# Keeping the split output- and query-projection panels in DRAM, and a gate matmul that writes with stride 4

## The chip, the cores and the metric

The kernel runs on one core of a Trainium2 chip. The metric is device microseconds (us) of one execution, as the median of several runs. The core's engines run at the same time, each through its own list of instructions in order: TensorE (PE, with its weight loads PEld), VectorE (DVE), ScalarE (ACT), GpSimd (POOL) and SyncE (SP), which issues most transfers. Transfers of SP and of POOL run on the same 16 DMA engines.

## The reference, cut to what matters

One layer, 1024 tokens of width 1024, float32. Attention in two head groups, then the output projection, then PEER: each token picks 16 of 16384 experts in each of 8 heads by product keys, and sums their one-neuron outputs.

```python
x = x + gt1 * (mixed @ w_out[l])
h2 = rms_norm(x, g_norm_ffn[l]) * (1.0 + sc2) + sh2
query = (ht @ w_query).reshape(t, PEER_HEADS, 2, PEER_HALF)
sub_scores = einsum('thpd,hpkd->thpk', query, sub_keys)
...                      # top 16 of each half, top 16 of their sums
experts = i1 * PEER_N_KEYS + i2
gates = softmax(top_vals)
act = gelu(einsum('td,thkd->thk', xb, expert_down[eb])) * gb
x = x + gt2 * einsum('thk,thkd->td', act, expert_up[eb])
```

## The kernel before, in words

Tokens are cut into block A (five tiles of 128) and block B (three tiles). The block-A tokens go through all 128x128 experts densely ("dense stage"); the block-B tokens gather their own experts' rows (`ring` tiles) beside it.

**Panels.** Products with large weights are made in two float32r halves: `wh` is the rounded weight panel (ACT, `split`), `wl` the rest (DVE, a subtraction in `low`), and `mm3` issues three matmuls for each piece. `Panels` loads a raw panel `wf` (128x1024, 512 KB), splits it one panel ahead of its use, and loads the next when `wf` is free. Two buffers hold `wh` and two `wl`. `w_out` has 8 panels, `w_q` 16; block A and block B each load and split all 24.

**Dense gates.** The dense stage needs, for each expert, the gates of all block-A tokens. Two ways build them:
- Tiles 0 and 1 (`scatter`): POOL adds each gate into the DRAM arrays `gds` by an indirect DMA of 128 single elements, 256 of them. They are issued in order, and each waits for the one issued eight before it. The first needs the first finished group of candidates of block A.
- Tiles 2 to 4 (`gbuild`): one-hot rows `ob` are compared on DVE, copied to `o2` (ACT) or scaled by the gate to `o1` (DVE), multiplied on PE (four matmuls of 128x128 into one PSUM bank), copied to `gt` (ACT), and after every 32 tokens `gt` (2 MB, one buffer) is stored to `gd`. There are 12 such stores.

**Order of the work.** The streams are merged by weights (`mrg`), and a scheduler then orders each engine's list. The stages that matter here: post A and route A (output projection and top-k of block A, beside the projections of block B), attention B, then the last merge, which runs post B, `post_b`, route B and `gbuild` together, then the dense stage, whose PE, DVE and ACT order is the code's own. A group of four experts loads its gates with `loadg`: `gg` from `gds` and `g4` from `gd`. The loads of the first group are issued on POOL, those of the second group on SP.

Of the kernel before, what the change touches and what calls it, by code (L numbers as in the profile page):

```python
# [11 lines left out]
F32 = mybir.dt.float32  # L12
F32R = mybir.dt.float32r
# [3 lines left out]
AF = mybir.ActivationFunctionType  # L17
# [3 lines left out]
P = 128  # L21
T = 1024
D = 1024
# [82 lines left out]
def tile_kernel(ctx: ExitStack, tc: tile.TileContext, x, ccol, w_ada, badac, bgt2, gcols, w_in, w_f, bf_, gout,  # L106
                w_out, w_q, keysT, edown, eup, wdense, gfin, out, dbg=None, stop=None):
    nc = tc.nc
    V, S, G, PE = nc.vector, nc.scalar, nc.gpsimd, nc.tensor
    dma = nc.sync.dma_start  # L110
# [3 lines left out]
    dram = ctx.enter_context(tc.tile_pool(name="dram", bufs=1, space=bass.MemoryType.DRAM))  # L114
# [38 lines left out]
    qsp = dram.tile([8, 3, P, T], F32R, name="qsp")  # L153
    ksp = dram.tile([8, 2, P, T], F32R, name="ksp")
    vsp = dram.tile([8, P, T], F32, name="vsp")
    gd = dram.tile([NPT * P // SB, P, NE * SB], F32, name="gd")
    gds = [dram.tile([NE * P * P, 1], F32, name="gds%d" % i) for i in range(NSC)]
    pidx = cst.tile([P, 1], F32, name="pidx")
# [2 lines left out]
    class Block:  # L161
        def __init__(self, t0, parts):
            self.t0, self.parts = t0, []
            i0 = 0
            for n in parts:
                self.parts.append((i0, n))
                i0 += n
            self.nt = i0
            self.ht = i0 * P
            self.nk = (t0 + i0) * P  # L170
            self.nq = 2 if t0 else 1
# [67 lines left out]
    def defer(fn, n=1):  # L239
        t_ = [n, fn]  # L240
        late.append(t_)
        return t_

    def force(t_):
        if t_ in late:
            late.remove(t_)
            t_[1]()
# [27 lines left out]
    def mrg(*streams, bg=()):  # L275
        live = [[q[0], float(q[1]), 0.0, q[2] if len(q) > 2 else 0] for q in streams + tuple(bg)]
        side = [q[0] for q in bg]
        need = len(streams)
        while need:
            for q in sorted(live, key=lambda q: q[2] / q[1]):  # L280
                c = adv(q)
                if c is None or c >= 0:
                    break
            assert c is None or c >= 0
            if c is None:
                live.remove(q)
                need -= not any(q[0] is g for g in side)
                continue
            q[2] += c
            tick(c)  # L290
            step()
        while late:
            late.pop(0)[1]()
        lead.clear()
# [17 lines left out]
    def split(dst_h, dst_l, src):  # L312
        S.activation(dst_h, src, AF.Copy)
        V.tensor_sub(dst_l, src, dst_h.bitcast(F32))

    class Panels:
        def __init__(self, pool, srcs, bufs=3, eng=V):
            self.eng = eng
            self.pool, self.src, self.bufs = pool, list(srcs), bufs
            self.ld, self.sp = [], []  # L320
            for _ in range(bufs - 1):
                self.load()
            self.split()

        def load(self):
            if self.src:
                w = self.pool.tile([P, D], F32, name="wf", tag="wf", bufs=self.bufs)
                dma(w, self.src.pop(0))
                self.ld.append(w)

        def split(self):
            if self.ld:
                w = self.ld.pop(0)
                wh = self.pool.tile([P, D], F32R, name="wh", tag="wh", bufs=2)
                wl = self.pool.tile([P, D], F32R, name="wl", tag="wl", bufs=2)
                S.activation(wh, w, AF.Copy)

                def low():
                    if self.eng is G:
                        G.tensor_sub(wl, w, wh.bitcast(F32))  # L340
                    else:
                        V.tensor_sub(wl, w, wh.bitcast(F32))

                self.sp.append((wh, wl, defer(low, LW)))
                self.load()

        def get(self):
            wh, wl, t_ = self.sp.pop(0)
            force(t_)
            self.split()  # L350
            return wh, wl

    def mm3(pt, wh, wl, hh, hl, cs, m=P, k0=0, k1=KD):
        for kd in range(k0, k1):
            c = slice(kd * m, (kd + 1) * m)
            PE.matmul(pt, wl[:, c], hh[:, kd, cs], start=kd == 0, stop=False)  # L356
            PE.matmul(pt, wh[:, c], hl[:, kd, cs], start=False, stop=False)  # L357
            PE.matmul(pt, wh[:, c], hh[:, kd, cs], start=False, stop=kd == KD - 1)  # L358
# [656 lines left out]
    def gbuild(ti, gp, alloc):  # L1015
        tp = alloc()
        for n, s_ in enumerate(cols3[ti]):
            PE.transpose(tp[:, n * P:(n + 1) * P], s_, identf)
        ib = gp.tile([P, 2, P], BF, name="ib", tag="ib", bufs=2)
        S.activation(ib, tp[:, :2 * P].rearrange("p (n t) -> p n t", n=2), AF.Copy)  # L1020
        gT = gp.tile([P, P], F32, name="gT", bufs=2)
        S.activation(gT, tp[:, 2 * P:3 * P], AF.Copy)
        io4 = gp.tile([P, P, 4], BF, name="io4", bufs=1)
        if ti == NSC:
            V.tensor_copy(io4, iof[:, :, None].to_broadcast([P, P, 4]))
            gio.append(io4)
        iob = gio[0][:, None].to_broadcast([P, 2, P, 4])

        def onehot(n, t):
            o = gp.tile([P, 2, P, 4], BF, name="ob%d" % n, tag="ob", bufs=3)  # L1030
            ids = ib[:, n, t:t + 8].rearrange("p (q t) -> p q t", t=4)[:, :, None, :]
            V.tensor_tensor(o, iob, ids.to_broadcast([P, 2, P, 4]), OP.is_equal)
            return o.rearrange("p q i t -> p q t i")

        for sb in range(P // SB):
            gt = gp.tile([P, NE, SB], F32, name="gt", tag="gt", bufs=GTB)
            for q in range(SB // 8):
                t = sb * SB + q * 8
                e2 = onehot(1, t)
                o2 = gp.tile([P, 2, 4, P], F32, name="o2", tag="o2", bufs=O2B)  # L1040
                S.activation(o2, e2, AF.Copy)
                e1 = onehot(0, t)
                o1 = gp.tile([P, 2, 4, P], F32, name="o1", tag="o1", bufs=O1B)
                gs = gT[:, t:t + 8].rearrange("p (q t) -> p q t", t=4)[:, :, :, None]
                V.tensor_tensor(o1, e1, gs.to_broadcast([P, 2, 4, P]), OP.mult)
                for q2 in range(2):
                    pg = alloc()
                    for r in range(4):
                        PE.matmul(pg[:, r * P:(r + 1) * P], o2[:, q2, r], o1[:, q2, r], start=True, stop=True)  # L1049
                    c_ = q * 8 + q2 * 4  # L1050
                    S.activation(gt[:, :, c_:c_ + 4].rearrange("p i t -> p t i"), pg.rearrange("p (t i) -> p t i", i=P),  # L1051
                                 AF.Copy)
                    yield GBC
            dma(gd[(ti - NSC) * (P // SB) + sb], gt.rearrange("p i t -> p (i t)"))

# [2 lines left out]
    st_hpa, st_pw, st_hpb, st_xp, st_ad, st_at, st_s3, st_gp = [ExitStack() for _ in range(8)]  # L1058

    def pool(stack, name, bufs=1, **kw):  # L1060
        return stack.enter_context(tc.tile_pool(name=name, bufs=bufs, reuse_waits="tile", **kw))
# [8 lines left out]
    def xtile(p_, b, name):  # L1070
        return p_.tile([P, b.nt, D], F32, name=name, tag="xr")
# [35 lines left out]
    am[0], ax[0] = ALS[0]()  # L1107
    s3p = pool(st_s3, "s3p", side="right")
    wop = [w_out[j] for j in range(KD)] + [w_q[j] for j in range(16)]
    opan = Panels(s3p, wop, bufs=2)  # L1110
    mrg((post(bA, mixA, lambda: xtile(xp, bA, "x1A"), opan), 60, HPB), (ad3, AD3), bg=((pp, PP3), (zr, ZR3)))
    rA = chain(post_b(bA), route(bA, opan))
    mrg((pp, PP4), (ad5, 10), bg=((rA, TOT_RA, HPC), (zr, 20)))
    for st_ in (st_ad, st_hpb, st_pw, st_xp):
# [8 lines left out]
    am[0], ax[0] = ALS[2]()  # L1123
    soft_rs[0] = RS2
    mb = pool(st_at, "mb")
    opan = Panels(s3p, wop, bufs=2)
    hp_[0] = pool(st_hpa, "hpc", 2)
    gp = pool(st_gp, "gp")
    mrg((chain(post(bB, mixB, lambda: xtile(mb, bB, "x1B"), opan), post_b(bB), route(bB, opan)), 150),
        (chain(*[gbuild(ti, gp, ptp) for ti in range(NSC, ND)]), TOT_G))  # L1130
    for st_ in (st_gp, st_hpa, st_at, st_xp, st_s3):
        st_.close()
# [310 lines left out]
```

## Time and profile before

| | |
|---|---|
| three runs | 3127.29, 3130.71 (median), 3133.5 us |
| the profiled execution | 3109.18 us, span 3107.4 us |
| mean granted clock of PE | 0.962 |
| busy: PE, DVE, ACT, POOL | 2864.6, 2561.8, 1213.5, 1587.9 us |

The span is the profiled stretch inside the execution's own time; 1.8 us lie around it. The profiled execution was 21.5 us (0.7%) shorter than the median of the three runs, so a difference read in the trace is added to that median. Busy shares are means over stages with different limits; which engine sets the pace is read stage by stage.

### The profile page before, as it was taken

Reading aid. Unit: us, or ns where it says so; the run is one execution under the profiler, and the core shown is the slowest. Engines: PE = TensorE matmul, PEld = TensorE weight load, DVE = VectorE, ACT = ScalarE, POOL = GpSimd, SP = SyncE. Lnnn points to the kernel's source line nnn. Section 1 sums busy time; section 2 is a strip of 40 time slices with the busy share of each in tenths; the row PEclk is TensorE's granted clock in tenths of the full one; section 3 lists DMA queues with packets and bytes.
Section 4 is the critical chain, followed back from the end, with each engine's and each line's share of the span. In section 5 each row is a group of like instructions: output and inputs, shape, how many; then the busy total and the mean of one; then the engine's idle time right before and its main releaser. Section 6 shows DMA issues by size and latency. Waiting matters only on the chain.

```text
span 3107.4 us, 47293 instructions
## 1 busy us (share of the span) xinstructions
PE 2864.6 (92%) x17213; PEld 2649.5 (85%) x17213; DVE 2561.8 (82%) x5226; ACT 1213.5 (39%) x2098; POOL 1587.9 (51%) x1089
## 2 busy tenths in 40 slices
PE   6999998989988891679999999999999999999997
PEld 4899998988888791679989989899898988999986
DVE  7677645999977693689889899898898988989996
ACT  5566745436767872332312213222122231222312
POOL 0000000077777677026566676665677656657771
PEclk9999999989979996889999999999999999999998
DMA  7998333465435553549999999999999999999995
GB/s 264 298 350 269 124 124 129 138 153 121 105 54 142 157 156 48 166 161 340 349 348 339 339 335 341 351 342 355 328 351 343 335 343 347 346 336 331 348 331 193
DMA packets 385593, 802.43 MB, mean 258 GB/s; under 512 B 66168, under 2 KB 208016, under 8 KB 383824
## 3 DMA queue, kind: packets, MB, share of 16 engines
q0 software_dynamic: 149984, 412.03, 39.4%
q1 hardware_dynamic: 235376, 387.39, 37.0%
q8 instruction: 135, 2.21, 0.3%
q14 instruction: 98, 0.80, 0.1%
HBM read 721.52 MB, written 77.76 MB: 257 GB/s over the span
## 4 chain that ended last, share of the span: by engine, by line
PE 36%; issue 18%; DVE 16%; POOL 14%; DMA 13%; ACT 4%; SPq 0%; POOLq 0%; DVEq 0%; ACTq 0%
DMA ring<-in_eup,e 7%; POOL ring L1193 7%; POOL ring L1206 6%; PE sp L356 3%; PE sp L358 3%; PE sp L357 3%; PE av L683 2%; PE proj L356 2%; PE proj L357 2%; PE proj L358 2%; POOL gds L1011 1%; PE po L1302 1%; PE po L1304 1%; PE po L1303 1%; DMA ring<-in_edown,e 1%
## 5 line engine op out<-in xcount | busy, mean ns | idle before, releaser
L1193 POOL DMA_INDIRECT ring<-in_edown,e x384 | 509.9, 1328 | 391.5 <-DVE ring L1195 223.4
L1206 POOL DMA_INDIRECT ring<-in_eup,e x384 | 573.0, 1492 | 263.6 <-DVE sacc L1211 173.9
L356 PE MATMUL sp<-hT,dl 128*128 128x320 f32 x2048 | 635.2, 310 | 18.0 <-ACT ge L1279 9.7
L357 PE MATMUL sp<-hT,dh 128*128 128x320 f32 x2048 | 634.4, 310 | 0.0
L358 PE MATMUL sp<-hT,dh 128*128 128x320 f32 x2048 | 634.4, 310 | 0.0
L1011 POOL DMA_INDIRECT gds<-g,e x256 | 457.4, 1787 | 312.3 <-DVE i L867 136.6
L1211 DVE SCALAR_TENSOR_TENSOR sacc<-ring,sdot,sacc 128x1024 f32<-128x1024 f32 x381 | 488.7, 1283 | 60.9 <-DMA ring<-in_eup,e 55.6
L1195 DVE SCALAR_TENSOR_TENSOR ring<-ring,sx 128x1024 f32<-128x1024 f32 x384 | 461.3, 1220 | 70.0 <-DMA ring<-in_edown,e 68.9
L356 PEld LDWEIGHTS sp<-hT,dl 128*128 128x128 f32 x2048 | 386.0, 188 | 20.6 <-ACT ge L1279 11.8
L1268 ACT ACTIVATE uh<-wfu 128x1024 fp32r<-128x1024 f32 x128 | 134.8, 1053 | 675.3 <-PE po L1304 675.3
L357 PEld LDWEIGHTS sp<-hT,dh 128*128 128x128 f32 x2048 | 386.1, 189 | 1.2
L358 PEld LDWEIGHTS sp<-hT,dh 128*128 128x128 f32 x2048 | 385.9, 188 | 0.0
L1302 PE MATMUL po<-ul,ch 128*128 128x512 f32 x768 | 303.7, 395 | 18.1 <-DVE accB L1311 10.3
L1279 ACT ACTIVATE ge<-sp 128x320 f32<-128x320 f32 x256 | 110.7, 433 | 498.7 <-PE sp L358 477.9
L1303 PE MATMUL po<-uh,ch 128*128 128x512 f32 x768 | 300.8, 392 | 0.0
L1304 PE MATMUL po<-uh,cl 128*128 128x512 f32 x768 | 300.6, 391 | 0.0
L1303 PE MATMUL pers<-uh,ch 128*128 128x512 f32 x512 | 199.6, 390 | 0.0
L1302 PE MATMUL pers<-ul,ch 128*128 128x512 f32 x512 | 199.5, 390 | 0.0
L1304 PE MATMUL pers<-uh,cl 128*128 128x512 f32 x512 | 199.2, 389 | 0.0
L1302 PEld LDWEIGHTS po<-ul,ch 128*128 128x128 f32 x768 | 145.3, 189 | 56.3 <-DVE accB L1311 18.7
L1049 PE MATMUL tp<-o,o 128*128 128x128 f32 x768 | 102.7, 289 | 93.2 <-ACT gt L1051 89.2
L302 POOL TENSOR_TENSOR i<-ms,mhalf 128x4 f32<-128x4 f32 (+1 forms) x16 | 22.4, 1399 | 324.1 <-DVE ms L300 324.1
(305 smaller groups left out, 6518.4 us busy)
## 6 DMA issues: line engine op xcount, KB each, us to landing
wfd<-in_wdense SPq DMA_DIRECT2D x128, 512.0 KB
wfu<-in_wdense SPq DMA_DIRECT2D x128, 512.0 KB
wa<-in_w_ada SPq DMA_DIRECT2D x96, 256.0 KB
wf<-in_w_in SPq DMA_DIRECT2D x48, 512.0 KB
gd<-gt SPq DMA_DIRECT2D x12, 2048.0 KB
g<-gd SPq DMA_DIRECT2D x31, 768.0 KB
gds<-zt SPq DMA_DIRECT2D x32, 512.0 KB
wf<-in_w_q SPq DMA_DIRECT2D x32, 512.0 KB
```

The source lines that it names most:

```text
L356: PE.matmul(pt, wl[:, c], hh[:, kd, cs], start=kd == 0, stop=False)
L357: PE.matmul(pt, wh[:, c], hl[:, kd, cs], start=False, stop=False)
L358: PE.matmul(pt, wh[:, c], hh[:, kd, cs], start=False, stop=kd == KD - 1)
L1011: G.indirect_dma_start(out=gds[i], out_offset=off, in_=b.g[:, c_:c_ + 1], in_offset=None, compute_op=OP.add)
L1193: G.indirect_dma_start(out=r, out_offset=None, in_=edown, in_offset=bass.IndirectOffsetOnAxis(ap=bs.e[:, c_:c_ + 1], axis=0))
L1195: (V.scalar_tensor_tensor(r, r, 1.0, sx, op0=OP.mult, op1=OP.mult, accum_out=s_[:, j:j + 1]))
L1206: G.indirect_dma_start(out=r, out_offset=None, in_=eup, in_offset=bass.IndirectOffsetOnAxis(ap=bs.e[:, c_:c_ + 1], axis=0))
L1211: (V.scalar_tensor_tensor(acc, r, s_[:, j:j + 1], acc, op0=OP.mult, op1=OP.add))
L1268: S.activation(k.uh, k.wfu, AF.Copy)
L1302: PE.matmul(po, k.ch[:, tcs], k.ul[:, ds_], start=c == 0 and (gi == 0 or not per), stop=False)
L1303: PE.matmul(po, k.ch[:, tcs], k.uh[:, ds_], start=False, stop=False)
L1304: PE.matmul(po, k.cl[:, tcs], k.uh[:, ds_], start=False, stop=c == CG - 1 and (gi == NG - 1 or not per))
```

## The change

A DRAM array `wsp` holds 24 pairs of split panels. Block A's `Panels` stores each `wh` and `wl` there after the split; block B's panels come from a new class, `Kept`, which loads the two halves (512 KB each, three buffers of each) and splits nothing. Apart from that, a gate matmul writes its 128 columns with a step of four elements into the PSUM bank, so that the copy to `gt` reads the bank in order and writes runs of four elements.

```diff
+    wsp = dram.tile([24, 2, P, D], F32R, name="wsp")
...
                 S.activation(wh, w, AF.Copy)
+                kp = self.keep.pop(0) if self.keep else None
 
                 def low():
...
+                    if kp is not None:
+                        for n_, t_ in enumerate((wh, wl)):
+                            dma(kp[n_].bitcast(F32), t_.bitcast(F32))
...
+    class Kept:
+        def __init__(self, pool, srcs, bufs=3):
+            self.pool, self.src, self.bufs, self.ld = pool, list(srcs), bufs, []
+            for _ in range(bufs - 1):
+                self.load()
+
+        def load(self):
+            if self.src:
+                src = self.src.pop(0)
+                t = [self.pool.tile([P, D], F32R, name=n_, tag=n_, bufs=self.bufs) for n_ in ("wh", "wl")]
+                for n_, t_ in enumerate(t):
+                    dma(t_.bitcast(F32), src[n_].bitcast(F32))
+                self.ld.append(t)
+
+        def get(self):
+            self.load()
+            return self.ld.pop(0)
...
-                        PE.matmul(pg[:, r * P:(r + 1) * P], o2[:, q2, r], o1[:, q2, r], start=True, stop=True)
+                        PE.matmul(pg.rearrange("p (i t) -> p i t", t=4)[:, :, r], o2[:, q2, r], o1[:, q2, r],
+                                  start=True, stop=True)
                     c_ = q * 8 + q2 * 4
-                    S.activation(gt[:, :, c_:c_ + 4].rearrange("p i t -> p t i"), pg.rearrange("p (t i) -> p t i", i=P),
-                                 AF.Copy)
+                    S.activation(gt[:, :, c_:c_ + 4], pg.rearrange("p (i t) -> p i t", t=4), AF.Copy)
...
-    opan = Panels(s3p, wop, bufs=2)
+    opan = Panels(s3p, wop, bufs=2, keep=[wsp[j] for j in range(24)])
...
-    opan = Panels(s3p, wop, bufs=2)
+    st_s3.close()
+    opan = Kept(pool(st_s3, "s3k", side="right"), [wsp[j] for j in range(24)], 3)
```

The order of POOL's list is the same in both kernels, and so is the order on PE, DVE and ACT up to post A and through the dense stage. In between, DVE has 24 subtractions fewer and ACT 24 copies fewer, and the scheduler places some rows of the last merge otherwise. On SP, in route A, before (a `w_q` panel among the stores of projection B; `kt` are the keys):

```order
L328 DMA wf<-in_w_q 128x1024
L532 DMA qsp<-pqa 128x384
L532 DMA qsp<-pqb 128x384
L835 DMA kt<-in_keysT 128x128
L532 DMA qsp<-pql 128x384
L504 DMA vsp<-vv 128x384
L328 DMA wf<-in_w_in 128x1024
L545 DMA ksp<-pka 128x384
L545 DMA ksp<-pkb 128x384
```

and at the same place of the change:

```order
L347 DMA wsp<-wh 128x1024
L347 DMA wsp<-wl 128x1024
L329 DMA wf<-in_w_q 128x1024
L555 DMA qsp<-pqa 128x384
L555 DMA qsp<-pqb 128x384
L858 DMA kt<-in_keysT 128x128
L555 DMA qsp<-pql 128x384
L527 DMA vsp<-vv 128x384
L329 DMA wf<-in_w_in 128x1024
L568 DMA ksp<-pka 128x384
L568 DMA ksp<-pkb 128x384
```

Two stores stand directly ahead of each load; the rest is in the same order. On SP at the start of the last merge (post B), before:

```order
L419 DMA x1B<-in_x 128x1024 x3
L1054 DMA gd<-gt 128x4096
L328 DMA wf<-in_w_out 128x1024 x4
L1054 DMA gd<-gt 128x4096
L328 DMA wf<-in_w_q 128x1024 x3
L1054 DMA gd<-gt 128x4096
L328 DMA wf<-in_w_q 128x1024
```

and of the change:

```order
L442 DMA x1B<-in_x 128x1024 x3
L1077 DMA gd<-gt 128x4096
L369 DMA wl<-wsp 128x1024 x2
L369 DMA wh<-wsp 128x1024 x3
L369 DMA wl<-wsp 128x1024 x2
L369 DMA wh<-wsp 128x1024
L1077 DMA gd<-gt 128x4096
L369 DMA wl<-wsp 128x1024
L369 DMA wh<-wsp 128x1024
```

Two loads of 512 KB take the place of one. On SP at the seam from the last merge to the dense stage, before (`gg` waits for the scatters; the two `gd` stores are the 11th and 12th; `wfd` and `wfu` are the dense stage's weights):

```order
L1244 DMA wfu<-in_wdense 128x1024
L1252 DMA gg<-gds_107 128x4x128
L1252 DMA gg<-gds_108 128x4x128
L1054 DMA gd<-gt 128x4096 x2
L1242 DMA wfd<-in_wdense 128x1024
L1254 DMA g_13860<-gd 128x12x128
L1242 DMA wfd<-in_wdense 128x1024
```

and of the change:

```order
L1268 DMA wfu<-in_wdense 128x1024
L1276 DMA gg<-gds_108 128x4x128
L1276 DMA gg<-gds_109 128x4x128
L1077 DMA gd<-gt 128x4096
L1266 DMA wfd<-in_wdense 128x1024 x2
L1077 DMA gd<-gt 128x4096
L1278 DMA g_13865<-gd 128x12x128
```

The two `gg` loads stand ahead of the last two `gd` stores in both; in the change two weight loads come between those stores. On DVE at that seam the subtractions `dl` of the first two experts stand 42 rows behind the last gate product `o` (L1045) before, and directly behind it (L1068) in the change:

```order
L889 MAX v_12810<-sr 128x8
L890 MAX_INDEX i_12811<-v_12810,sr 128x8
L1068 TENSOR_TENSOR o_12688<-ob_12686,gT 128x1024
L978 SCALAR_TENSOR_TENSOR bq<-pos,bq 128x128
L1287 TENSOR_TENSOR dl<-wfd,dh 128x1024 x2
```

## Rows read from the trace of the kernel before

**Rows 1.** Page: the span in 40 equal slices, busy tenths.

```profile
PE   6999998989988891679999999999999999999997
...
POOL 0000000077777677026566676665677656657771
```

**Rows 2.** Busy time by stretch: window, length, PE, PEld, DVE, ACT, POOL, PEclk, DMA share, GB/s.

```profile
930.00:1187.00 257.00, 225.00 (x1493) 213.23 (x1492) 208.35 (x576) 197.46 (x269) 176.85 (x93) 0.95 0.55 152
1187.00:1259.00 72.00, 0.00 (x0) 0.00 (x0) 7.08 (x51) 0.64 (x2) 52.30 (x35) 0.50 0.32 44
```

**Rows 3.** Chain that ended last, around the seam: start, us, what.

```profile
1244.02 5.45 DMA gds<-g,e x2
...
1249.96 8.81 DMA gd<-gt
...
1269.96 7.39 DMA gd<-gt
...
1277.97 10.95 DMA g<-gd
```

**Rows 4.** Timeline of SP's queue at the seam.

```profile
1167.21 0.56 SPq L1244 DMA_DIRECT2D wfu<-in_wdense  x1
1247.08 2.79 SPq L1252 DMA_DIRECT2D gg<-gds  x2
```

**Rows 5.** The scatters (line L1011): times ns min/median/max, first and last start.

```profile
L1011 POOL DMA_INDIRECT gds<-g,e x256: 1539/1552/5116, 614.3 to 1245.9; - x128
```

**Rows 6.** Scatters by stretch: POOL busy (count), PEclk, DMA share, GB/s.

```profile
614.00:690.00 76.00, 56.50 (x33) 0.95 0.55 128
690.00:940.00 250.00, 182.15 (x103) 0.87 0.47 100
940.00:1187.00 247.00, 168.07 (x89) 0.97 0.57 158
1187.00:1246.00 59.00, 49.23 (x33) 0.50 0.22 0
```

**Rows 7.** POOL's waits in those four stretches: total us, times, longest.

```profile
POOL gds L1011 <- DMA gds<-g,e: 11.5, 11, 2.5
...
POOL gds L1011 <- DMA gds<-g,e: 48.2, 34, 3.3
...
POOL gds L1011 <- DMA gds<-g,e: 57.9, 23, 5.8
...
POOL gds L1011 <- issue: 9.8, 32, 0.3
```

**Rows 8.** Timeline of POOL: first and last of eight long waits.

```profile
1010.79 1.63 POOL L1011 DMA_INDIRECT gds<-g,e  x1 [5.51 <-DMA gds<-g,e]
...
1172.17 1.55 POOL L1011 DMA_INDIRECT gds<-g,e  x1 [5.83 <-DMA gds<-g,e]
```

**Rows 9.** Page: DMA issues, KB each.

```profile
gd<-gt SPq DMA_DIRECT2D x12, 2048.0 KB
...
wf<-in_w_q SPq DMA_DIRECT2D x32, 512.0 KB
```

**Rows 10.** Timeline of SP: first and last of five `w_q` loads after 614.

```profile
617.58 0.33 SPq L328 DMA_DIRECT2D wf<-in_w_q  x1
...
680.57 0.33 SPq L328 DMA_DIRECT2D wf<-in_w_q  x1
```

**Rows 11.** Groups by line and form, last merge: count, busy, mean ns.

```profile
L342 DVE TENSOR_TENSOR wl<-wf,wh 128x1024 fp32r<-128x1024 f32 x22 | 26.9, 1224 | 8.6 <-ACT wh L336 8.3
L1051 ACT ACTIVATE gt<-tp 128x512 f32<-128x512 f32 x96 | 99.1, 1122 | 101.3 <-DMA gd<-gt 79.5 <-PE tp L1049 19.4 <-issue 2.2
L856 ACT ACTIVATE scs<-proj 128x384 f32<-128x384 f32 x16 | 8.0, 502 | 9.3 <-DVE sr L865 6.8 <-PE proj L854 1.3 <-issue 1.2
```

**Rows 12.** Waits of PE at the seam.

```profile
PE sp L356 <- DVE dl L1263: 7.2, 1, 7.2
```

**Rows 13.** Gate matmuls (L1049) alone, last merge: PE, PEld, PEclk, DMA.

```profile
930.00:1187.00 257.00, 94.23 (x720) 89.54 (x720) 0.95 0.55 152
```

More of the change, by code (lines that the diff above doesn't have):

```diff
@@ L316, in tile_kernel, with __init__ @@
     class Panels:
-        def __init__(self, pool, srcs, bufs=3, eng=V):
-            self.eng = eng
+        def __init__(self, pool, srcs, bufs=3, eng=V, keep=None):
+            self.eng, self.keep = eng, keep and list(keep)
             self.pool, self.src, self.bufs = pool, list(srcs), bufs
```

## The prediction

> **What bounds the kernel now.** I read the page's slices first [rows 1]: PE is busy nine tenths and more almost everywhere, but in the 16th slice (1165 to 1243 us) it falls to one tenth while POOL goes on. The stretches say the same [rows 2]: in the last merge, 930 to 1187, PE works 225.0 of 257 us, DVE 208.4 and ACT 197.5; from 1187 to 1259 all three have next to nothing, and POOL is busy 52.3 us of the 72. Behind that lies the dense stage, in which the slices show PE full to the end; it needs the gates, so it is shifted as one piece with the moment at which they are there.
>
> The chain of waits names what ends last in that hole [rows 3]: the last scatters (L1011), 5.45 us until they land, then the 11th `gd` store (8.81), the last gate copies, the 12th store (7.39) and the `g4` load (10.95). SP shows why the stores are so late [rows 4]: it has nothing to do after 1167 but wait for `gg<-gds`, which waits for the scatters, and the two `gd` stores stand behind that in its list. `gt` has one buffer, so `gbuild` stands still too. So the last merge is done early and waits; the scatters set the seam.
>
> The scatters run from 614.3 to 1245.9 [rows 5]. One takes 1.55 us, and undisturbed the next follows after 0.31 (9.8 us over 32 [rows 7]): 1.86 us, or 476 us for 256. They take 633. Of the excess 157, some 97 are waits for an earlier scatter's transfer (11.5 + 48.2 + 57.9 us in 68 waits [rows 7], less 0.3 each that would pass anyway), and 59 are longer descriptor writing (the busy times of [rows 6] add up to 456 us, 256 times 1.55 is 397). With the other transfers gone, at 0 GB/s, 33 pass in 59 us; at 158 GB/s, 89 in 247, one in 2.78 us [rows 6].
>
> **The change part by part.**
>
> *Work taken from the last merge.* 24 subtractions `wl` (22 of them inside, 26.9 us of DVE [rows 11]) and as many copies `wh` on ACT go, and each of 96 copies to `gt` should fall from 1.12 us towards 0.67, the 0.50 us of a 128x384 copy in order [rows 11] times 4/3. All this is worth nothing directly: the cover is the 72 us from 1187 to 1259. It only makes that hole longer. One part reaches the scatters: their descriptor writing in this stretch takes 168.07/89 = 1.89 us instead of 1.55, 30 us in all, beside a DVE busy 208 us. If the excess follows DVE's work, 26.9/208 of 30 is 4 us less. Bounds 0 and 10 (a rival below). I take -4.
>
> *Transfers added.* A panel half is 512 KB, 0.52 MB [rows 9]. Stores: 24 pairs, 25 MB. Those of the first 17 panels fall before 614, when no scatter runs; five of the panel loads that they stand in front of come after 614 [rows 10], and the last two pairs have no load behind them, so seven pairs, 7.3 MB, meet the scatters. Loads: 24 pairs instead of 24 single panels, 12.6 MB more, all while scatters run. Together 19.9 MB.
>
> Their price for the scatters comes from the stretches [rows 6, 7], as waiting beyond 0.3 us divided by megabytes moved. 614 to 690: 8.2 us for 76 us x 128 GB/s = 9.7 MB, 0.84 us/MB. 690 to 940: 38 for 25 MB, 1.5. 940 to 1187: 51 for 39 MB, 1.3; but there eight waits, 37.7 us together, first and last in [rows 8], each follow a 2 MB `gd` store [rows 9] by some 10 us; without them 16 us remain for the 18 MB that are not `gd`, 0.87. The new transfers are like the 512 KB ones, so I take 0.87: 19.9 x 0.87 = +17 us. Bounds: 1.5 us/MB, the dearest stretch, gives +30; 0 if each pair is over before the scatter eight places on looks (eight times 1.86 is 15 us).
>
> The Trainium skill, "DMA: Bandwidth & Descriptors", section "Queues, rings and completion order", says that a DMA engine alternates between queues a packet at a time. Long waits behind `gd` stores alone agree with that [rows 8]; by this rule panel halves, a quarter of a `gd` store each, would cost less per megabyte than the mean, and the sum would be nearer to its lower bound.
>
> *Stores in post A and route A.* Here, 390 to 690, PE is busy eight to nine tenths and more [rows 1]. Each pair is issued at the moment at which SP would have issued the panel's load anyway, since both wait for `wl`, so SP stands still no longer, and a buffer is wanted again only a panel later. DVE's list is the same as far as the first finished candidates. I take 0 for the start of the scatters; upper bound +5, if the 1.6 MB per panel, 6 us at a `gd` store's rate (2.1 MB in 8.8 or 7.4 us [rows 3]), overrun the short panels of post A by a microsecond each.
>
> *The seam.* Behind the scatters' end come eight copies to `gt`, of which about five follow one another on the chain: 5 x 0.45 = 2 us less. `dl` moves up by 42 rows of DVE, which run in the hole instead; PE no longer waits 7.2 us for it [rows 12], but then stands before the third expert until `g4` is there, so at most 2 us remain. Against it, two weight loads now lie ahead of the 12th `gd` store: 1 MB, up to 4 us. Bounds -7 and +4; I take -2.
>
> Sum: -4 + 17 + 0 - 2 = +11 us. The profiled execution would go from 3109.2 to 3120, and the median of the runs, 21.5 us above it, from 3130.7 to 3142.
>
> **The rivals.**
>
> *No change.* The pairs are spread, in route A one per 16 us [rows 10], and the eight places of the scatters absorb them; price under 0.5 us/MB. Then +10 at most, minus 4 to 8 from DVE and the seam: within 6 us of before, 3131. For it: 68 of 256 scatters wait at all. Against: the 614-690 stretch has no `gd` store and still 0.84 us/MB.
>
> *Faster.* The last merge ends some 30 us earlier (it is 257 us long and loses 27 us of DVE and, in the copies to `gt` alone, 43 of ACT), and for those 30 us scatters pass at 1.86 instead of 2.78 us: 16 instead of 11, worth 10 us. With the seam's 2 that is 3119, if the transfers cost nothing. It decides where the price per megabyte is under 0.3 us. Against: the transfers do not vanish with the work, and in the merge most of the waiting is theirs.
>
> *The stepped matmul outputs.* No row here shows a matmul that writes with a step. The gate matmuls take 94.2 us of PE in the merge [rows 13]. PE has 32 us free there and the 72 us behind it [rows 2]: 104 us. Twice the time (+94) would just fit, and cost some 6 us at the seam, where eight banks are still to be filled; from there on it decides: at three times (+188) the merge would end 84 us after 1259, 3131 + 84 + 11 = 3226.
>
> The Trainium skill, "SBUF — State Buffer", section "Door 1: The DMA port swizzle", says that PSUM has lines of 8 bytes and that matmuls slow down significantly with any access that is not contiguous. With four-byte elements at a step of 16 bytes every column would open a line of its own; by that rule this rival comes true, with a factor that the page doesn't give.
>
> **How the numbers follow.** About 6 us, 0.2%, is what a measurement of this kernel can tell from no change. Forecast (slower by 6 to 40 us, with a doubled matmul inside it): 0.47. No change: 0.27. Faster: 0.18. Stepped outputs at three times or more: 0.08. Slower is 0.47 + 0.08 = 0.55. The range leaves out the last case and the edges: from 3119, the faster rival, to 3131 + 30 + 5 + 6 = 3172, the upper bounds of transfers, start and a doubled matmul. The forecast's own range is 3137 to 3172.
>
> **What would show it.** Right: the scatters still start near 614 and end 10 to 25 us later; the count of waits for `gds` transfers is up in 614-690 and in the merge; PE's hole behind the merge is longer than 72 us. `gt` copies near 0.67 us. Wrong: scatters ending at or before 1246; a first scatter clearly off 614; gate matmuls far above 94 us, with PE full up to the seam; or a dense stage of another length, of which I expect none, since its list is unchanged.

## The result, and the profile after

The change makes the kernel slower: 3153.14 us (median of 4 runs, 3148.88 to 3153.91) against 3132.11 us (4 runs), a ratio of 1.0066 with a 95% interval of 1.0049 to 1.0083. That is +21 us. The profiled execution of the change took 3153.91 us (span 3152.1), which is typical of it. The one of before, from which all the rows ahead of the prediction come, is one of the shorter ones, 23 us under the median; so the difference between the two traces, 45 us, is not the size of the change.

The page's slices of the changed kernel, busy tenths of 40 equal slices, beside [rows 1]:

```profile
PE   5899998989898990379999999999999999999997
...
POOL 0000000066685558306656767566577656656771
```

The shape is the same: TensorE (PE) falls to nothing once, before the dense stage, while POOL goes on. The stretch in which PE stands still has become longer. Here are the last merge, in a window of the same 257 us that is shifted by 13, and the hole behind it up to the last scatter (columns as in [rows 2]):

```profile
943.00:1200.00 257.00, 216.30 (x1488) 210.39 (x1488) 198.88 (x661) 143.06 (x247) 153.23 (x85) 0.93 0.65 197
1200.00:1288.50 88.50, 0.00 (x0) 0.00 (x0) 0.00 (x0) 0.00 (x0) 72.94 (x48) 0.50 0.22 0
```

DVE and ACT have less to do in the merge, as intended, and the reader can see that nothing comes of it: PE then waits for 88.5 us until the last scatter. In that stretch almost nothing else moves (0 GB/s), 48 scatters are still to be issued, and before it was 33 [rows 6]. The scatters themselves (L1034, was L1011), minimum, median and maximum of one in ns, first and last start; then four stretches of them that answer to [rows 6], and the waits in the first three, [rows 7]:

```profile
L1034 POOL DMA_INDIRECT gds<-g,e x256: 1540/1553/4471, 624.0 to 1288.5; - x128
```

```profile
624.00:700.00 76.00, 51.07 (x30) 0.95 0.68 192
700.00:950.00 250.00, 176.08 (x96) 0.87 0.49 114
950.00:1230.00 280.00, 171.35 (x98) 0.89 0.61 181
1230.00:1290.00 60.00, 50.22 (x33) 0.50 0.22 0
```

```profile
POOL gds L1034 <- DMA gds<-g,e: 19.1, 10, 3.3
...
POOL gds L1034 <- DMA gds<-g,e: 47.2, 25, 4.9
...
POOL gds L1034 <- DMA gds<-g,e: 83.6, 30, 6.3
```

They now take 664.5 us from the first to the last, against 631.6. The waits for an earlier scatter's transfer have grown where the new transfers are: from 11.5 to 19.1 us in the first stretch, in which the moved bytes rose from 128 to 192 GB/s, and from 57.9 to 83.6 in the merge. In between they stayed (48.2, 47.2), and in the quiet last stretch 33 scatters pass in the same time as before.

The seam behind the last scatter, from the chain that ended last (start, us, what), beside [rows 3]:

```profile
1286.62 5.44 DMA gds<-g,e x2
...
1292.55 8.95 DMA gd<-gt
...
1311.45 9.42 issue
...
1336.49 0.63 PE sp L379
```

The third row is the 12th `gd` store, issued at 1310.95, until the `g4` load goes out at 1320.84. PE is steady 48.0 us after the last scatter (1336.49 less 1288.5), as in the kernel before (1293.76 less 1245.9, 47.9). From there to the end it is 1815.6 us, against 1813.6. So only the moment of the last scatter differs. Of the 42.6 us by which it is later in this pair of traces, 9.7 are a later first scatter and 32.9 a longer chain of scatters. That is more than the change costs in the medians; a trace of a typical execution stands in for the kernel before in the table below.

### The profile page after: what moved, and what is told of

Its sections match the earlier page's. It is cut to its first block, busy times and chain, and to the rows that moved or that the text cites. A ratio compares the mean times of both kernels' runs of the same rounds, so it can differ in the third digit from the quotient of the medians.

```text
span 3152.1 us, 47374 instructions
## 1 busy us (share of the span) xinstructions
PE 2861.0 (91%) x17213; PEld 2650.9 (84%) x17213; DVE 2534.2 (80%) x5202; ACT 1157.8 (37%) x2074; POOL 1581.3 (50%) x1089
## 4 chain that ended last, share of the span: by engine, by line
issue 25%; PE 21%; POOL 20%; DMA 16%; DVE 15%; ACT 3%; SPq 0%; POOLq 0%; DVEq 0%; ACTq 0%
POOL ring L1217 10%; DMA ring<-in_eup,e 7%; POOL ring L1230 6%; POOL gds L1034 4%; DMA gds<-g,e 3%; DMA wa<-in_w_ada 2%; PE proj L379 2%; PE av L706 2%; PE proj L380 2%; PE proj L381 2%; PE sp L379 1%; PE sp L380 1%; PE sp L381 1%; DVE prs L650 1%; DMA ring<-in_edown,e 1%
## 5 line engine op out<-in xcount | busy, mean ns | idle before, releaser
L1034 POOL DMA_INDIRECT gds<-g,e x256 | 448.7, 1753 | 353.9 <-DMA gds<-g,e 150.2
L379 PEld LDWEIGHTS sp<-hT,dl 128*128 128x128 f32 x2048 | 386.2, 189 | 22.8 <-ACT ge L1303 21.5
L1072 PEld LDWEIGHTS tp<-o,o 128*128 128x128 f32 x768 | 98.4, 202 | 142.0 <-ACT gt L1075 138.0
```

The source lines that it names most:

```text
L1034: G.indirect_dma_start(out=gds[i], out_offset=off, in_=b.g[:, c_:c_ + 1], in_offset=None, compute_op=OP.add)
L1072: PE.matmul(pg.rearrange("p (i t) -> p i t", t=4)[:, :, r], o2[:, q2, r], o1[:, q2, r], start=True, stop=True)
```

## The experiments

Twelve kernels in three groups. Each group was timed beside the kernel before on one chip; its medians there were 3125.0, 3122.0 and 3123.9 us.

**One part at a time.** Four kernels: the panels alone, the stride alone, the stores alone, the doubled loads alone.

`panels_only` keeps the gate matmul and the gate copy of before:

```diff
-PE.matmul(pg.rearrange("p (i t) -> p i t", t=4)[:, :, r], o2[:, q2, r], o1[:, q2, r],
-          start=True, stop=True)
+PE.matmul(pg[:, r * P:(r + 1) * P], o2[:, q2, r], o1[:, q2, r], start=True, stop=True)
...
-S.activation(gt[:, :, c_:c_ + 4], pg.rearrange("p (i t) -> p i t", t=4), AF.Copy)
+S.activation(gt[:, :, c_:c_ + 4].rearrange("p i t -> p t i"), pg.rearrange("p (t i) -> p t i", i=P),
+             AF.Copy)
```

> The change without its stride part: block A stores the split panels, block B loads them, and the gate copies stay as they were. Theory (the added traffic lengthens the chain of scatters, what the merge saves is hidden): all of the loss is here, +17 to +25 us on the median of before, last scatter 25 to 35 us after that of before, seam from the last scatter to steady matmuls still near 48 us. Rival (the stride part, which relieves ScalarE, changes what collides with the scatters): half or less of the loss here, +0 to +10 us.

`stride_only` is the kernel before with that edit the other way round.

> Only the gate matmuls and the gate copies are changed, the panels stay as before. Theory: the gate copies take 0.60 us and the 96 of them 58 us instead of 99, all of it hidden by the hole before the dense stage, so the time stays within 5 us of before (-4 to +2). Rival (the stride part carries half of the loss): +8 to +15 us. A second rival (ScalarE sets the end of the last merge and the seam follows the merge): -10 us or more.

`stores_only` is `panels_only` with block B's panels loaded raw and split again:

```diff
-st_s3.close()
-opan = Kept(pool(st_s3, "s3k", side="right"), [wsp[j] for j in range(24)], 3)
+opan = Panels(s3p, wop, bufs=2)
```

> Block A stores the split panels, nobody loads them: block B loads and splits the raw panels as before; gate copies as before. Theory: of 25.2 MB of stores about 7 to 12 MB run beside the scatters, at 0.9 to 1.5 us per MB: +6 to +15 us, with the scatters between 630 and 750 us slower and those after 900 us as before. Rival (stores cost nothing, since the scatters wait for few long transfers there; the doubled loads carry all): within 4 us of before.

`loads_only` is `panels_only` with one pair stored and all 24 pairs loaded from it:

```diff
-opan = Panels(s3p, wop, bufs=2, keep=[wsp[j] for j in range(24)])
+opan = Panels(s3p, wop, bufs=2, keep=[wsp[0]] + [None] * 23)
...
-opan = Kept(pool(st_s3, "s3k", side="right"), [wsp[j] for j in range(24)], 3)
+opan = Kept(pool(st_s3, "s3k", side="right"), [wsp[0]] * 24, 3)
```

> Block B loads both halves for each panel and splits nothing, as in the change, but only the first panel is stored, once, and all 24 pairs of loads read that one pair (block B so multiplies with panel 0 everywhere; the work and the bytes loaded are those of the change). Gate copies as before. Theory: 12.6 MB more loads in the last merge, partly paid back by the lighter VectorE: +7 to +15 us, scatters between 940 and 1190 us slower (waits for the transfer of an earlier scatter up by 20 us or more). Rival (the loads are free and the stores carry the loss): within 4 us of before, or faster by up to 10 us since VectorE's 24 subtractions are gone.

Measured, as a ratio to before, with the difference of the medians: panels 1.0058 (1.0039 to 1.0076), +20 us; stride 1.0007 (0.9994 to 1.0021), +1; stores 1.0039 (1.0026 to 1.0052), +10; loads 1.0058 (1.0045 to 1.0071), +16. The loss is in the panels, and both halves of it carry some; the loads cost a microsecond more than was expected. How the 20 us divide is not shown: the halves add up to 26, and by the ratios the loads alone lose as much as the whole. The waits for scatters between 620 and 760 us, where the stores of the last panels run, for `stride_only`, then `stores_only`, then `loads_only` (total us, times, longest):

```profile
POOL gds L1011 <- DMA gds<-g,e: 31.6, 24, 3.4
```

```profile
POOL gds L1034 <- DMA gds<-g,e: 39.8, 25, 3.5
```

```profile
POOL gds L1034 <- DMA gds<-g,e: 29.3, 21, 3.4
```

And the same three between 950 and 1200 us, where block B's panels are loaded:

```profile
POOL gds L1011 <- DMA gds<-g,e: 64.3, 23, 6.5
```

```profile
POOL gds L1034 <- DMA gds<-g,e: 62.6, 24, 5.9
```

```profile
POOL gds L1034 <- DMA gds<-g,e: 83.6, 31, 6.9
```

Each part lengthens the waits where its own transfers run, and nowhere else. The table collects the profiles; `stride_only` stands for the kernel before, since its profile is of a typical execution. Waits are those on scatters' transfers in three stretches, then the time that all 256 spend writing descriptors, the time from the first to the last start, and from the last start to the end of the span.

| kernel | 620-760 | 760-950 | 950-1200 | writing | first to last | last to end |
|---|---|---|---|---|---|---|
| `stride_only` | 31.6 | 25.4 | 64.3 | 463.6 | 642.1 | 1861.5 |
| `stores_only` | 39.8 | 22.8 | 62.6 | 457.5 | 641.8 | 1864.9 |
| `loads_only` | 29.3 | 29.6 | 83.6 | 450.4 | 649.1 | 1863.4 |
| `panels_only` | 38.1 | 30.1 | 83.2 | 448.0 | 658.1 | 1866.5 |
| the change | 41.3 | 29.3 | 83.6 | 448.7 | 664.5 | 1863.6 |

From the last scatter to the end it is the same time within 5 us in all of them. The profile of `stores_only` is of the fastest of its five runs, 5 us under its median, so its waits show the place of the loss, but its chain not the whole size. Nor is a small difference in the column "first to last" to be read: with none of the new transfers it is 631.6 us in the kernel before, 642.1 in `stride_only` and 650.0 in `gg_before` (below).

**The seam alone.** If the scatters set the dense stage's start, a shorter seam should move both kernels alike. `gg_before` and `gg_after` issue the second group's gate loads on GpSimd, so that the last two `gd` stores no longer stand behind them on SyncE:

```diff
-    dma = nc.sync.dma_start if gi else G.dma_start
+    dma = nc.sync.dma_start if gi > 1 else G.dma_start
```

> The kernel before, with the second set of gate loads (gg, g4) issued by GpSimd behind the first set instead of by SyncE ahead of the last two gd stores. Theory (the last scatter releases the seam, but about 25 of the 48 us from it to the steady matmuls come from the two gd stores queued behind a load that waits for the scatters): the last scatter stays where it was, the gate matmuls end near 1190 to 1200, and the dense stage is steady 15 to 30 us after the last scatter: -15 to -35 us on before. Rival (the seam is set by the g4 load and the refill, whatever the order): within 5 us of before.

> The change, with the second set of gate loads issued by GpSimd in the same way. Theory (the scatter chain still releases the dense stage, and the added traffic lengthens it): it gains as much as the kernel before does by this, and stays 15 to 28 us slower than that one (the loss of the change itself). Rival (the loss came from the two late gd stores at the seam): 5 us or less between the two.

`gg_before` is faster than before, 0.9945 (0.9930 to 0.9960), 3106.2 us. `gg_after` took 3129.6 us: against `gg_before` it still loses 23 us, as much as the change loses. The chain of waits of `gg_before` behind its last scatter at 1273.1 (start, us, what):

```profile
1271.21 4.74 DMA gds<-g,e x2
...
1276.24 0.84 POOL gg L1252 x2
...
1278.49 6.96 DMA g<-gd
...
1290.30 0.64 PE sp L356
```

The `gd` stores are gone from the chain, and 17.2 us after the last scatter PE goes on, against 47.9. From the last scatter to the end it is 1835 us instead of 1861. That is 26 us, of which the medians show 16. In this execution the last scatter came 10 us later than in `stride_only` (1263.4); whether by chance, or since weight loads and gate stores now run beside the last scatters (51 GB/s from 1200 to 1273), was not tried. `gg_before` is the fastest kernel with a full result in this study, faster than both kernels, and it has nothing of the change.

**Half the scatters, first way.** `npt4_before` and `npt4_after` build one tile more with one-hot matmuls, so that 128 scatters go, all into one table (`NPT = 4`; a few small buffers share their place to make room).

> The kernel before with 128 scatters instead of 256: tile 1's gates too are built with one-hot matmuls in the last merge (four tiles there instead of three; a few small buffers are shared to make room). Theory (the scatters set the seam): the last scatter comes before 1100 us, and the seam follows the last merge, which is 20 to 40 us longer; the dense stage starts 10 to 40 us earlier: -10 to -40 us on before. Rival (VectorE, with a third more one-hot work, carries the merge past the old seam): +0 to +25 us.

> The change with 128 scatters in the same way. Theory (what the change saves in the last merge is real but hidden behind the scatters): with the scatters off the path it becomes visible, and this kernel is 5 to 20 us faster than its counterpart of before. Rival (the added traffic costs the merge as much as the lighter VectorE and ScalarE give, or the merge is bound by TensorE): within 4 us of its counterpart, or slower.

This went against the theory: 1.0034 (1.0022 to 1.0047) and 1.0083 (1.0066 to 1.0101), both slower than before, and the change 16 us slower than its counterpart. The scatters of `npt4_before`, their line and what POOL waited for (us, times, longest), show that the theory's premise did not hold:

```profile
L1012 POOL DMA_INDIRECT gds<-g,e x128: 1539/1552/3766, 624.4 to 1192.4; - x128
```

```profile
POOL gds L1012 <- DMA gds<-g,e: 319.1, 122, 8.2
```

Half as many scatters take 568 us, nearly as long as 256 did: 122 of 128 wait for a transfer. They still end late, and in `npt4_after` later yet, at 1214.0, with 347.2 us of waits in 122. Their end also weighs more here than before, since six `gd` stores instead of two stand behind the `gg` load that waits for it; SyncE of `npt4_before`:

```profile
1196.37 36.96 SPq L1055 DMA_DIRECT2D gd<-gt  x3
...
1252.99 35.60 SPq L1055 DMA_DIRECT2D gd<-gt  x3
```

PE is steady 119.7 us after the last scatter instead of 47.9. The order of POOL's list has the reason for the waits, given here with what each row waits for. In the kernel before, the second and third scatter:

```
43 L1011 DMA gds1_108<-g0_4708,e0_4707 2097152x1 [waits DMAHW6_49,DMAHW7_49,DMAHW2_49,DMAHW1_49]
44 L1011 DMA gds0_107<-g0_4708,e0_4707 2097152x1 [waits DMASW0_49]
```

In `npt4_before`, the second:

```
43 L1012 DMA gds0_107<-g0_4691,e0_4690 2097152x1 [waits DMASW0_49]
```

Lanes are taken in turn, and lane 0 is the first scatter's. A scatter adds into its table, so it waits until the one before it into the same table has landed: two places back with two tables, which alternate without exception in the kernel before, and one place back with one. It is not eight places, as the description of the kernel and the prediction have it.

**Four tables.** `tab4_before` and `tab4_after` test that directly: every second slot goes to two further tables.

```diff
-gds = [dram.tile([NE * P * P, 1], F32, name="gds%d" % i) for i in range(NSC)]
+gds = [dram.tile([NE * P * P, 1], F32, name="gds%d" % i) for i in range(2 * NSC)]
...
-G.indirect_dma_start(out=gds[i], out_offset=off, ...
+G.indirect_dma_start(out=gds[i + NSC * (k % 2)], out_offset=off, ...
```

> The kernel before, with its 256 scatters spread over four tables instead of two: every second slot goes to two further tables, which are zeroed too (16.8 MB more stores ahead of the scatters) and never read, so half of the scattered gates are left out of the result. Theory (each scatter waits for the one before it into the same table, two places back; with four tables, four places back): the 117 to 121 us of waits for scatters fall below 50 us, the last scatter comes 70 us earlier or more after the first, and the dense stage starts 30 to 70 us earlier, unless the extra zeroing delays the first scatter by as much. Rival (the waits are for the queue's lane eight places back): the waits stay above 100 us and the scatters last as long as before.

> The change with four tables in the same way (half of the scattered gates are left out of the result). Theory (the traffic costs by making the scatters' transfers late, and only a short slack lets that through): waits below 60 us, and the loss against the counterpart of before falls from 21 us to 10 us or less, or turns into a gain of up to 10 us where the last merge then sets the seam. Rival (the traffic also slows the descriptor writing or the merge): the loss stays at 15 us or more.

The waits of the first, then of the second:

```profile
L1011 POOL DMA_INDIRECT gds<-g,e x256: 1542/1557/4904, 664.0 to 1214.6; - x128
...
  DMA gds<-g,e: 16.6, 13
```

```profile
L1034 POOL DMA_INDIRECT gds<-g,e x256: 1542/1554/3629, 659.4 to 1212.3; - x128
...
  DMA gds<-g,e: 16.4, 16
```

The one before into the same table is now four places back, for 249 of the 256. With that slack the waits fall from some 120 us to 16, and the scatters take 551 and 553 us: the same with and without the change's transfers. The zeroing delays the first scatter by 40 us, and still the kernels are faster than before, 3082.5 and 3077.2 us. The last scatter still sets the seam: from it to the end it is 1861 and 1858 us, as in the first table. The loss of 21 us has become a gain of 5: in the traces the first scatter is 4.6 us earlier, the chain 2.3 longer and the rest 2.9 shorter. The new transfers still run beside the scatters (207 GB/s instead of 151 between 660 and 760 us, 203 instead of 138 between 950 and 1200), so it is not the later start of the scatters that spares them; the transfers have next to no price left.

**Half the scatters, second way.** `half_before` and `half_after` leave out every second slot's scatter and keep the two tables:

```diff
-                if i < NSC:
+                if i < NSC and k % 2 == 0:
```

> The kernel before without every second slot's scatter: 128 scatters, still over two tables (the dense tiles 0 and 1 so lack half of their gates). Theory (the scatters set the seam): the last scatter comes between 900 and 1000 us, the dense stage follows the end of the last merge and starts near 1220: -65 to -90 us on before. Rival (something else holds the seam near 1290): within 10 us of before.

> The change without every second slot's scatter, in the same way. Theory (the whole loss goes through the scatters, and the savings of the last merge are real but hidden): with the scatters off the path it is 5 to 15 us faster than its counterpart of before. Rival (the added traffic slows the merge itself, or the merge is bound by TensorE): between 4 us faster and slower.

Here the last scatter starts at 975.6 and 974.5, some 200 us before the last merge is over, and sets nothing. Medians 3047.1 and 3034.1 us: the change is 13 us **faster** than its counterpart. The chains at the seam, first of `half_before`, then of `half_after`:

```profile
1199.32 1.96 ACT gt L1051 x2
1201.30 6.69 DMA gd<-gt
...
1208.60 12.33 DMA g<-gd
...
1225.78 0.42 PE sp L356
```

```profile
1186.30 3.43 PE tp L1072 x16
1189.75 0.30 ACT gt L1075
1190.32 10.38 issue
...
1216.31 0.64 PE sp L379
```

("issue" is again the last `gd` store, then the `g4` load.) The last copy to `gt` is done 11 us earlier with the change, and PE goes on 9.5 us earlier. This is the saving of the last merge, which the change really makes, and which the full kernel hides behind its scatters. How much of it comes from the panels and how much from the cheaper copies was not tried.

## Why the prediction was right and where its sizes were off

The direction and the place were right, and so was the mechanism but for its slack: the added transfers make scatters wait, and the scatters set the seam. 3153 us lies in the range, but that is little proof, since it reaches from 3119, a gain, to 3172; the forecast's own range, 3137 to 3172, holds it too. The forecast of +11 us should have been +21. By its steps:

*Work taken from the last merge: nothing directly.* Right, and shown twice: `stride_only` is within the measurement of before although its gate copies fall to 600 ns, and the saving appears, 13 us, as soon as the scatters are out of the way (`half_after`). The copies became cheaper than the 0.67 us I took:

```profile
L1075 ACT ACTIVATE gt<-tp 128x512 f32<-128x512 f32 x96 | 55.8, 601 | 172.6 <-DMA gd<-gt 125.3 <-PE tp L1072 42.7 <-issue 4.6
```

*A lighter DVE shortens descriptor writing: -4 us.* Not borne out as it stands. With two tables, 256 scatters write for 448.0 to 450.4 us without the subtractions (`panels_only`, `loads_only`, `gg_after`, the change) and for 455.2 to 463.6 with them (`gg_before`, before, `stores_only`, `stride_only`): about -10. With four tables, where hardly a scatter waits, nothing is saved. The scatters of `tab4_before`, with the subtractions, and of `tab4_after`, without (busy us, mean ns):

```profile
L1011 POOL DMA_INDIRECT gds<-g,e x256 | 461.6, 1803 | 227.8 <-DVE i L867 136.9
```

```profile
L1034 POOL DMA_INDIRECT gds<-g,e x256 | 465.2, 1817 | 225.6 <-DVE i L890 136.3
```

So it is not shown that the lighter DVE shortens the writing. A wait is counted from the end of the writing before it; where scatters wait, a writing that ends sooner makes the wait for the same landing longer. Part of the -10 can be the other side of the next term.

*Transfers added: +17 us.* Measured by the waits, this is the term that failed. In the table's columns, kernels with stores wait 9 us more in 620-760 (38.1 to 41.3 against 29.3 and 31.6), and kernels with doubled loads 20 us more in 950-1200 (83.2 to 83.6 against 62.6 and 64.3), 29 us in all. The stretch between adds 0 to 6: 29.3 to 30.1 against 22.8 and 25.4 in the table, but `gg_before`, without the loads, has 29.8 there too. For the price, the bytes of the same stretches: the stores raise 142 GB/s to about 190 over 140 us, 6.7 MB, and the loads raise 156 to 203 over 250 us, 11.8 MB (and 79 to 90 over 190 us, 2.1 MB). So 29 us for 18.5 MB, 1.6 us/MB. The amount, 19.9 MB, was right (20.6); the price is not 0.87 but about the upper bound of 1.5. I had got 0.87 by taking the waits behind `gd` stores out of the merge and calling the rest the price of small transfers. That was also done unevenly: the bytes of all ten stores of the stretch were taken out, but the waits of eight. The first two stores, issued at 952.75 and 975.52, are followed by long waits as well:

```profile
959.58 1.55 POOL L1011 DMA_INDIRECT gds<-g,e  x1 [3.78 <-DMA gds<-g,e]
...
981.67 1.55 POOL L1011 DMA_INDIRECT gds<-g,e  x1 [3.97 <-DMA gds<-g,e]
```

With these out too, the price would have been 0.47 us/MB, further off; that it was 0.87 is in part luck. The stretch 690 to 940 [rows 6, 7], which has no `gd` store and cost 1.5, was the better row. By it the term is +30 and the sum +24.

The two terms have to be read together. The measured sizes, -10 and 29 to 35, give +19 to +25 where -4 and +17 gave +13. The scatters of the change take 22 us longer than those of `stride_only`, and those of `panels_only`, timed in the same group, 16 us: for 20.6 MB that is 0.8 to 1.1 us/MB, shorter writing included. If that writing is only the other side of the longer waits, 0.87 was a fair price and the -4 is the step that failed; if it is a saving of its own, the price is. The runs do not decide between the two.

The second fault lies under the first: *eight places of slack*. The slack is two places, 3.7 us at 1.86 us a scatter, and most of that is used up. From issue to landing, a scatter of `stride_only` takes:

```profile
DMA to landing us min/median/max: 2.9/3.4/10.7
```

In the median 0.3 us are left. That is why a delay of a few microseconds passes on at once. The rival "no change", which rests on those eight places, has no ground, and should have had less than 0.27.

The Trainium skill, "DMA: Bandwidth & Descriptors", section "Queues, rings and completion order", has an engine take its queues in turn, packet by packet. From that I said that panel halves would cost less per megabyte than the mean and the sum would be nearer its lower bound. By the waits the price went the other way, 1.6 us/MB against a mean of 1.3 in the merge before; with the shorter writing included it is 0.8 to 1.1, so these runs do not settle it.

*Stores in post A and route A: 0.* Right. The first scatter of the change is at 624.0, 10 us later than [rows 5], but this is the early execution of before: in `stride_only`, which has no stores, it is at 621.3, and in `panels_only` at 620.9.

*The seam: -2 us.* 0 in its place; both sides of it can be read. From the 11th `gd` store's landing (1301.50) to the issue of the 12th it now takes 9.5 us instead of 11.2, the cheaper copies. The 12th then takes 9.9 us to the `g4` load instead of 7.5, behind the two weight loads.

*The dense stage is unchanged.* Right, within 2 us.

The rival "faster" wanted the last merge to end 30 us earlier and the transfers under 0.3 us/MB. With the scatters away the merge ends 11 us earlier, and the price is well above that, 0.8 to 1.6. The rival of the stepped outputs is refuted. The gate matmuls, which write every fourth element of a bank:

```profile
L1072 PE MATMUL tp<-o,o 128*128 128x128 f32 x768 | 102.3, 287 | 139.4 <-ACT gt L1075 135.4 <-ACT o L1064 1.8 <-DVE o L1068 1.3
```

In the kernel before they took 102.7 us, 289 ns each. The Trainium skill, "SBUF — State Buffer", section "Door 1: The DMA port swizzle", expects a significant slowdown of matmuls for any access to PSUM that is not contiguous; for these float32 matmuls of 128 columns with a step of 16 bytes, the trace shows none. Nor is the chain at the seam slower for it: 16 of these matmuls take 3.79 us there in both kernels (from 1259.92 before, from 1302.23 in the change).

What stays open: how the stores come to cost 10 us in the medians when the one profile of `stores_only`, of the shortest of its runs, shows a chain of scatters no longer than that of `stride_only`, and `half_after`, with the same stores, one no longer than `half_before` (351 against 353 us); whether the shorter descriptor writing is a saving of its own; and why descriptor writing varies by 6 us between `stride_only` and `stores_only`, which have the same work on DVE.

## What to carry to other kernels

Work saved in a stage that is followed by a wait is worth nothing, and if it was paid for with transfers, what counts is what these do to the chain behind which the stage waits. Before pricing a chain of small DMAs, find out which earlier one each of them really waits for: two places of slack let most delays through, four absorbed nearly all of them. Whoever takes a cause out of a stretch has to take out all of its waits with all of its bytes; where that cannot be done cleanly, the stretch's whole price per megabyte is the safer one.

## What the runs showed of the hardware

These are times beside this kernel's other transfers. Accumulating scatters of 128 single floats into one table, each of which the program makes wait for the one before it, take 4.4 us each (568 us for 128); into two tables in turn 2.5 us (642 us for 256); into four 2.2 us (551 us for 256), of which 1.8 are descriptor writing.

An ACT copy of 128x512 float32 out of PSUM took 1122 ns when it wrote single floats 128 bytes apart [rows 11], and 601 ns when it wrote runs of four; it reads the bank in order in both kernels.

A float32 matmul of 128 columns took 289 ns when it wrote a PSUM bank in order, and 287 ns when it wrote every fourth element.
